# The up projection of an MLP by seven block products instead of eight

## The chip, the cores and the metric

The kernel runs on one core of one Trainium2 chip. The metric is device time in microseconds (us) of one execution, lower is better. Engines are named as in the profile: PE is TensorE's matmul, PEld its weight load, DVE is VectorE, ACT is ScalarE, POOL is GpSimd, SP issues DMAs.

## The reference, cut to what matters

One encoder block on 16 learned tokens and 512 real ones, width 2048, all in float32:

```python
h = rms_norm(h_res, norm1_g[l])
proj = h @ w_in[l]                       # 2048 x 6144
# ... short convolution on one half, neighbourhood attention on the other: mix
h_res = h_res + mix @ w_out[l]           # 2048 x 2048
h = rms_norm(h_res, norm2_g[l])
h_res = h_res + jnp.square(jax.nn.relu(h @ w_up[l])) @ w_down[l]   # 2048 x 8192, 8192 x 2048
out = rms_norm(h_res, final_norm_g)      # the 512 real tokens are returned
```

The change touches the line with `w_up` and `w_down`.

## The kernel before, in words

Every large matmul works on float32 values that are split in two: a rounded part (`hi`, written by ACT) and the remainder (`lo`, subtracted by DVE). A product is then three matmuls: hi by hi, hi by lo, lo by hi (`mm3`, lines 599 to 602, and lines 670 to 672 for the up projection). Weights arrive in slabs of 128 x 1024 values (512 KB) through `load` (SP's queue, tile `raw`), and `split` (lines 175 and 176) makes `whi` and `wlo` of them. Rings of buffers let a few slabs be loaded and split ahead of PE.

The stages stand one behind the other: projections with attention, projections with the convolution (tiles `mm_u`, `mm_c`, `mm_b`), the output projection (tiles `o_a`, `o_c`, lines 626 to 643), then the MLP. While the output projection runs, the residual stream `acc` is transposed 128 columns at a time (`transpose_h2`, tile `p2t`) and kept as `h2_hi` and `h2_lo`: 16 blocks of 128 model columns by 512 tokens.

The MLP goes in 8 chunks of 1024 hidden columns (`ch`). A chunk first makes its hidden columns: for each pair of 128-column blocks, 16 steps over the model width, each with two weight blocks and three matmuls of 128 x 512 (lines 670 to 672: 3072 matmuls in all). ACT takes relu out of PSUM, DVE squares, both split the result into `a_hi` and `a_lo`, which stay in SBUF. Then the chunk's share of the down projection follows, in four parts of 512 columns, 96 matmuls of 128 x 512 each (lines 600 to 602), and DVE adds the four banks into `acc` (line 706). PSUM has two groups of four banks (`mm`, `aux`) that take turns. The last part of the last chunk (`dl`) ends with the final norm and the stores.

The order of instructions on each engine is set by a scheduler that simulates the program; engines then run their own queues strictly in that order and wait for each other by semaphores.

Of the kernel before, what the change touches and what calls it, by code (L numbers as in the profile page):

```python
# [8 lines left out]
F32 = mybir.dt.float32  # L9
# [86 lines left out]
def hybrid_block_kernel(  # L96
# [23 lines left out]
    wp = ctx.enter_context(tc.tile_pool(name="wp", bufs=1, side="left"))  # L120
    psum = ctx.enter_context(tc.tile_pool(name="psum", bufs=4, space=bass.MemoryType.PSUM))
# [30 lines left out]
    def load(src, name):  # L152
        pool, bufs = wring["raw"].next()
        raw = pool.tile([P, SLAB], F32, tag="raw", name=f"raw_{name}", bufs=bufs)
        nc.sync.dma_start(raw, src)
        return raw

    def part_tiles(name):
        pool, bufs = wring["split"].next()
        return [pool.tile([P, SLAB], F32R, tag=t, name=f"{t}_{name}", bufs=bufs) for t in ("whi", "wlo")]  # L160
# [61 lines left out]
    with tc.tile_pool(name="p0", bufs=1, side="left") as p0:  # L222
        wring["raw"] = Ring((wp, 3, 3))
        wring["split"] = Ring((wp, 3, 2), (p0, 2, 2))
# [73 lines left out]
        wring["split"] = Ring((wp, 3, 3))  # L298
# [36 lines left out]
        wring["raw"] = Ring((wp, 3, 3))  # L335
# [242 lines left out]

    accp = ctx.enter_context(tc.tile_pool(name="accp", bufs=1, side="right"))
    acc = [accp.tile([P, D], F32, name=f"acc{t}") for t in range(NT)]  # L580
    for t in range(NT):
        nc.sync.dma_start(acc[t], x_v[t])
    h2p = tc.alloc_tile_pool(name="h2p", bufs=1, side="right")
    h2_hi = h2p.tile([P, KT, SEQ], F32R, name="h2_hi")
    h2_lo = h2p.tile([P, KT, SEQ], F32R, name="h2_lo")
    sq2 = h2p.tile([P, NT, 4], F32, name="sq2")
    rs2 = accp.tile([P, NT], F32, name="rs2")
# [19 lines left out]
    tags = ["mm", "aux"]  # L607
    turn = 0

    def transpose_h2(g):  # L610

        for t in range(NT):

            junk = h2p.tile([P, 960], mybir.dt.bfloat16, tag="junk", name=f"junk{g}_{t}")[:, :512]
            nc.scalar.activation(
                junk, acc[t][:, g * 512 : (g + 1) * 512], AF.Square, accum_out=sq2[:, t, g : g + 1]
            )
        for kt in range(4 * g, 4 * g + 4):
            pt = bank("aux", f"p2t{kt}")
            for t in range(NT):  # L620
                nc.tensor.transpose(
                    pt[:, t * P : (t + 1) * P], in_=acc[t][:, kt * P : (kt + 1) * P], identity=ident
                )
            split(h2_hi[:, kt, :], h2_lo[:, kt, :], pt, scale=g2T[:, kt : kt + 1])

    for g in range(4):
        c0 = g * 512
        for nm, xs, row, rs in halves:
            bs = [bank("mm" if nm == "a" else "aux", f"o_{nm}{c0}_{t}") for t in range(NT)]
            for s0 in range(0, 8, 2):  # L630
                wh, wl = slab(w_out[g, (row // P + s0) // 2], 512, f"o{nm}{c0}_{s0}")
                for k in range(2):
                    kt = s0 + k
                    for t in range(NT):
                        ts = slice(t * P, (t + 1) * P)
                        mm3(bs[t], xs[kt][0][:, ts], xs[kt][1][:, ts], wh[:, k, :], wl[:, k, :], kt == 0, kt == 7)
            for t in range(NT):
                a = acc[t][:, c0 : c0 + 512]
                nc.vector.scalar_tensor_tensor(a, bs[t], rs[:, t : t + 1], a, op0=ALU.mult, op1=ALU.add)

            if nm == "a" and g > 0:
                with tc.high_priority():
# [12 lines left out]
    wring["split"] = Ring((wp, 3, 3), (wp2, 3, 3))
    mp = ctx.enter_context(tc.tile_pool(name="mp", bufs=1, side="left"))
    tags = ["mm", "aux"]
    turn = 0
    for ch in range(NCHUNK):
        a_hi, a_lo = [], []  # L660
        for f in range(0, FCH, 2):
            bs = [bank(tags[turn], f"u{ch}_{f}_{i}") for i in range(2)]
            for s0 in range(0, KT, 4):
                wh, wl = slab(w_up[(ch * FCH + f) // 2, s0 // 4], 256, f"up{ch}_{f}_{s0}")
                for k in range(4):
                    kt = s0 + k
                    xh, xl = h2_hi[:, kt, :], h2_lo[:, kt, :]
                    for i in range(2):
                        h, l = wh[:, k, i * P : (i + 1) * P], wl[:, k, i * P : (i + 1) * P]
                        nc.tensor.matmul(bs[i], lhsT=h, rhs=xh, start=kt == 0, stop=False)  # L670
                        nc.tensor.matmul(bs[i], lhsT=h, rhs=xl, start=False, stop=False)  # L671
                        nc.tensor.matmul(bs[i], lhsT=l, rhs=xh, start=False, stop=kt == KT - 1)  # L672
            for i in range(2):
                r = mp.tile([P, SEQ], F32, tag="r", name=f"r{ch}_{f}_{i}", bufs=2)
# [135 lines left out]
```

## Time and profile before

| | |
|---|---|
| median of 3 runs | 2207.97 us (2207.5 to 2208.98) |
| the profiled execution | 2208.89 us, its span 2207.1 us |
| PE busy | 2192.9 us, 99% |
| DVE busy | 934.1 us, 42% |
| ACT busy | 652.2 us, 30% |
| granted TensorE clock | 0.998 of full speed |

The span runs from the first instruction to the last, and 1.8 us of the profiled execution lie outside it. Busy time says how long an engine had at least one instruction under way; on PE several matmuls are under way at once, so the duration of one and the distance from one start to the next are two different numbers.

### The profile page before, as it was taken

What the parts mean: (1) busy time and instruction counts of PE and PEld (TensorE: products, weight loads), DVE (VectorE), ACT (ScalarE), POOL (GpSimd) and SP (SyncE); (2) the same over time, 40 slices, a digit from 0 to 9 for tenths busy, and PEclk for the clock granted to TensorE, in tenths of its full rate; (3) what the DMA queues carried; (4) which work ended last, traced back from release to release, by engine and by line L of the source; (5) the groups of instructions that cost most, each with busy time, mean ns of one, the idle gap of its engine ahead of it and who ended that gap; (6) DMA issues with size and microseconds to landing.
All of it is one profiled execution on the core that took longest, in us unless ns stands there. A gap on an engine that the chain in (4) does not pass through costs nothing.

```text
span 2207.1 us, 27384 instructions
## 1 busy us (share of the span) xinstructions
PE 2192.9 (99%) x11348; PEld 1885.8 (85%) x11348; DVE 934.1 (42%) x1354; ACT 652.2 (30%) x984; POOL 143.3 (6%) x250
## 2 busy tenths in 40 slices
PE   9999999999999999999999999999999999999998
PEld 8999999999988888888888888888888888888887
DVE  6777666344334443333333333333333333333334
ACT  6455444222213333213212212212312212221323
POOL 0432221111100000000000000000000000000001
PEclk9999999999999999999999999999999999999999
DMA  5332222332363243333333333333333333333332
GB/s 196 81 91 77 82 82 77 96 95 89 95 172 91 91 143 96 96 96 98 99 100 96 96 95 96 97 100 100 96 96 96 96 97 100 99 96 96 96 105 77
DMA packets 77873, 219.00 MB, mean 99 GB/s; under 512 B 24292, under 2 KB 24372, under 8 KB 77108
## 3 DMA queue, kind: packets, MB, share of 16 engines
q1 hardware_dynamic: 77748, 217.24, 32.8%
q8 instruction: 89, 1.46, 0.3%
q14 instruction: 36, 0.29, 0.0%
HBM read 213.02 MB, written 4.19 MB: 98 GB/s over the span
## 4 chain that ended last, share of the span: by engine, by line
PE 99%; DMA 0%; ACT 0%; DVE 0%; SPq 0%; issue 0%; ACTq 0%; POOLq 0%; POOL 0%; DVEq 0%
PE u L670 11%; PE u L672 11%; PE u L671 11%; PE d L602 10%; PE d L601 10%; PE d L600 10%; PE mm_k L201 1%; PE mm_v L201 1%; PE mm_k L202 1%; PE mm_v L202 1%; PE mm_k L204 1%; PE mm_c L204 1%; PE mm_v L204 1%; PE mm_u L204 1%; PE mm_q L204 1%; PE mm_u L201 1%
## 5 line engine op out<-in xcount | busy, mean ns | idle before, releaser
L671 PE MATMUL u<-h_lo,whi_up 128*128 128x512 f32 x1024 | 398.4, 389 | 0.0
L672 PE MATMUL u<-h_hi,wlo_up 128*128 128x512 f32 x1024 | 398.4, 389 | 0.0
L670 PE MATMUL u<-h_hi,whi_up 128*128 128x512 f32 x1024 | 398.4, 389 | 0.0
L600 PE MATMUL d<-whi_dn,ah 128*128 128x512 f32 x992 | 385.9, 389 | 0.0
L601 PE MATMUL d<-wlo_dn,ah 128*128 128x512 f32 x992 | 385.9, 389 | 0.0
L602 PE MATMUL d<-whi_dn,al 128*128 128x512 f32 x992 | 385.9, 389 | 0.0
L176 DVE TENSOR_TENSOR wlo_up<-raw_up,whi_up 128x1024 fp32r<-128x1024 f32 x128 | 156.7, 1225 | 370.0 <-ACT whi_up L175 369.9
L176 DVE TENSOR_TENSOR wlo_dn<-raw_dn,whi_dn 128x1024 fp32r<-128x1024 f32 x124 | 151.9, 1225 | 369.3 <-ACT whi_dn L175 369.3
L175 ACT CAST whi_up<-raw_up 128x1024 fp32r<-128x1024 f32 x128 | 134.7, 1053 | 430.1 <-PE u L671 234.3
L175 ACT CAST whi_dn<-raw_dn 128x1024 fp32r<-128x1024 f32 x124 | 130.5, 1053 | 429.8 <-PE d L602 309.1
L672 PEld LDWEIGHTS u<-h_hi,wlo_up 128*128 128x128 f32 x1024 | 192.2, 188 | 40.0
L671 PEld LDWEIGHTS u<-h_lo,whi_up 128*128 128x128 f32 x1024 | 192.2, 188 | 39.9
L670 PEld LDWEIGHTS u<-h_hi,whi_up 128*128 128x128 f32 x1024 | 192.2, 188 | 39.8
L601 PEld LDWEIGHTS d<-wlo_dn,ah 128*128 128x128 f32 x992 | 186.2, 188 | 38.7
L600 PEld LDWEIGHTS d<-whi_dn,ah 128*128 128x128 f32 x992 | 186.2, 188 | 38.7
L602 PEld LDWEIGHTS d<-whi_dn,al 128*128 128x128 f32 x992 | 186.2, 188 | 38.6
L706 DVE SCALAR_TENSOR_TENSOR acc<-d,rs,acc 128x512 f32<-128x512 f32 x124 | 86.7, 750 | 38.9 <-PE d L602 38.9
L719 POOL TENSOR_TENSOR e<-sq 128x1 f32<-128x1 f32 x4 | 2.5, 632 | 1522.3 <-ACT junk L710 1522.3
L678 DVE TENSOR_TENSOR r<-r 128x512 f32<-128x512 f32 x64 | 44.1, 689 | 104.7 <-ACT r L677 104.7
L677 ACT ACTIVATE r<-u 128x512 f32<-128x512 f32 x64 | 38.3, 598 | 124.8 <-PE u L672 124.8
L201 PE MATMUL mm_k<-h_hi,whi_k 128*128 128x272 f32 (+1 forms) x256 | 70.0, 288 | 1.2 <-ACT whi_k L175 1.2
L201 PE MATMUL mm_v<-h_hi,whi_v 128*128 128x272 f32 (+1 forms) x256 | 69.1, 285 | 0.4 <-ACT whi_v L175 0.4
(222 smaller groups left out, 3383.1 us busy)
## 6 DMA issues: line engine op xcount, KB each, us to landing
raw_up<-in_w_up_dram SPq DMA_DIRECT2D x128, 512.0 KB
raw_dn<-in_w_down_dram SPq DMA_DIRECT2D x124, 512.0 KB
raw_q<-in_w_in_dram SPq DMA_DIRECT2D x16, 512.0 KB
raw_u<-in_w_in_dram SPq DMA_DIRECT2D x16, 512.0 KB
raw_c<-in_w_in_dram SPq DMA_DIRECT2D x16, 512.0 KB
raw_b<-in_w_in_dram SPq DMA_DIRECT2D x16, 512.0 KB
raw_oa<-in_w_out_dram SPq DMA_DIRECT2D x16, 512.0 KB
raw_oc<-in_w_out_dram SPq DMA_DIRECT2D x16, 512.0 KB
```

The source lines that it names most:

```text
L175: nc.scalar.copy(hi, src)
L176: nc.vector.tensor_tensor(lo, src, hi.bitcast(F32), op=ALU.subtract)
L201: nc.tensor.matmul(b, lhsT=wh, rhs=cols(h_hi, kt), start=kt == 0, stop=False)
L202: nc.tensor.matmul(b, lhsT=wh, rhs=cols(h_lo, kt), start=False, stop=False)
L204: last = nc.tensor.matmul(b, lhsT=wl, rhs=cols(h_hi, kt), start=False, stop=kt == KT - 1)
L600: nc.tensor.matmul(o, lhsT=ah, rhs=wh, start=start, stop=False)
L601: nc.tensor.matmul(o, lhsT=ah, rhs=wl, start=False, stop=False)
L602: nc.tensor.matmul(o, lhsT=al, rhs=wh, start=False, stop=stop)
L670: nc.tensor.matmul(bs[i], lhsT=h, rhs=xh, start=kt == 0, stop=False)
L671: nc.tensor.matmul(bs[i], lhsT=h, rhs=xl, start=False, stop=False)
L672: nc.tensor.matmul(bs[i], lhsT=l, rhs=xh, start=False, stop=kt == KT - 1)
L706: nc.vector.scalar_tensor_tensor(a, bs[t][:, :n], rs2[:, t : t + 1], a, op0=ALU.mult, op1=ALU.add)
```

## The change

The up projection is cut into 2 x 2 blocks three ways: the model width into pairs of 128 columns (8 pairs `m`), the hidden width into pairs of 128 columns (32 groups `n` of 256), the tokens into two halves of 256. Strassen's scheme (in Winograd's form) makes the four output blocks of a group from seven block products per pair instead of eight. Each product is one weight block of 128 x 128 times one operand of 128 x 256, again as three matmuls (lines 760 to 762 of the kernel after): 32 groups x 8 pairs x 7 products x 3 = 5376 matmuls of 128 x 256.

The sums that the scheme needs are made outside PE. `combine_h2` takes the place of `transpose_h2`: it scales the transposed blocks, makes four sums of them and splits all seven operands, for the 8 pairs. They lie in `sobuf` and in the tiles `xa` and `xc`, which the output projection has finished with by then. `up_slab` does the same for weights: per slab (two pairs) three sums on DVE into `tsum`, and splits of the plain blocks (`q`) and of the sums (`wsp`, 1024 columns). `up_out` combines the banks of a group by DVE, ACT applies relu and square, and the group's 512 KB go to DRAM (`a_d`). `acc` goes to DRAM too (POOL's queue), and its SBUF holds `tsum` and `q` meanwhile. The tokens are scaled before the sums (`token_scale`).

The down projection is now a phase of its own: `acc` and the groups come back from DRAM, each group is split, and the same 3072 matmuls of 128 x 512 follow.

```diff
-    def transpose_h2(g):
...
+    def combine_h2(g, tag):
+        for m in (2 * g, 2 * g + 1):
+            for e in range(2):
+                pt = bank(tag, f"p2t{2 * m + e}")
...
+                nc.vector.scalar_tensor_tensor(
+                    dst, two(pt), g2T[:, 2 * m + e : 2 * m + e + 1], two(s_bc), op0=ALU.mult, op1=ALU.mult
                 )
+            for o, a, b, op in ((4, 7, 3, ALU.subtract), (6, 0, 7, ALU.subtract), (5, 4, 0, ALU.subtract), (2, 1, 5, ALU.add)):
+                nc.vector.tensor_tensor(xq[:, o, :], xq[:, a, :], xq[:, b, :], op=op)
+            for i, j, v in places[m]:
+                split(v[:, :, 0, :], v[:, :, 1, :], xq[:, i:j, :])
+        nc.gpsimd.dma_start(acc_d[g], accs[g])
...
+    def up_slab(n, s):
+        raw = load(w_up[n, s], f"up{n}_{s}")
+        w, t = by4(raw), by4(TS.next())
+        q_hi, q_lo = (by4(v, 3) for v in Q3.next())
+        split(q_hi, q_lo, w[:, :, 1:4, :])
+        b12 = free_ap(raw[:, 0:1], [[512, 2], [0, 2], [1, P]])
+        nc.vector.tensor_tensor(t[:, :, 0:2, :], b12, w[:, :, 1:3, :], op=ALU.add)
+        nc.vector.tensor_tensor(t[:, :, 2, :], t[:, :, 0, :], w[:, :, 2, :], op=ALU.add)
+        nc.vector.tensor_tensor(t[:, :, 3, :], t[:, :, 2, :], w[:, :, 3, :], op=ALU.add)
+        t_hi, t_lo = (by4(v) for v in part_tiles(f"up{n}_{s}"))
+        split(t_hi, t_lo, t)
+        return (q_hi, q_lo), (t_hi, t_lo)
+
+    def up_step(bs, n, s):
+        both = up_slab(n, s)
+        for k in range(2):
+            m = 2 * s + k
+            for q, (sm, w, x, b, c) in PROD.items():
+                o = bs[b][:, c * HT : (c + 1) * HT]
+                h, l = (v[:, k, w, :] for v in both[sm])
+                xh, xl = (operand[m][x][:, i, :] for i in range(2))
...
+                nc.tensor.matmul(o, lhsT=h, rhs=xh, start=first, stop=False, skip_group_check=True)
+                nc.tensor.matmul(o, lhsT=h, rhs=xl, start=False, stop=False, skip_group_check=True)
+                nc.tensor.matmul(o, lhsT=l, rhs=xh, start=False, stop=m == NPR - 1, skip_group_check=True)
+
+    def up_out(bs, n):
+        e, u = E.next()
...
+        nc.scalar.copy(u[:, 0, :], bs[2][:, :HT])
+        nc.vector.tensor_tensor(u[:, 1, :], bs[0][:, :HT], u[:, 0, :], op=ALU.add)
+        nc.vector.tensor_tensor(e[:, 0, :], bs[2][:, HT:], u[:, 1, :], op=ALU.add)
+        nc.vector.tensor_tensor(e[:, 1, :], bs[3][:, :HT], u[:, 1, :], op=ALU.subtract)
+        nc.vector.tensor_tensor(e[:, 2, :], bs[3][:, :HT], e[:, 0, :], op=ALU.subtract)
+        nc.vector.tensor_tensor(e[:, 3, :], bs[0][:, HT:], u[:, 0, :], op=ALU.add)
+        nc.vector.tensor_tensor(e[:, 0:2, :], two(bs[1]), e[:, 0:2, :], op=ALU.add)
+        nc.scalar.activation(e, e, AF.Relu)
+        nc.scalar.activation(e, e, AF.Square)
+        nc.scalar.dma_start(a_d[n], e.rearrange("p s c -> p (s c)"))
...
+    accs = acc_tiles()
+    for g in range(4):
+        nc.gpsimd.dma_start(accs[g], acc_d[g])
...
+        for n in range(4 * ch, 4 * ch + 4):
+            r = AR.next()
+            nc.sync.dma_start(r, a_d[n])
+            both = A.next()
+            split(both[:, 0:1024], both[:, 1024:2048], r)
```

The first place is PE in the up projection. Before, one weight block of a slab meets `h2_hi`, `h2_lo` and again `h2_hi`, 512 tokens wide:

```order
L670 MATMUL u_2_0_8033<-h_hi,whi_up_2_12_8127 128x512
L671 MATMUL u_2_0_8033<-h_lo,whi_up_2_12_8127 128x512
L672 MATMUL u_2_0_8033<-h_hi,wlo_up_2_12_8128 128x512
L670 MATMUL u_2_1_8034<-h_hi,whi_up_2_12_8127 128x512
L671 MATMUL u_2_1_8034<-h_lo,whi_up_2_12_8127 128x512
L672 MATMUL u_2_1_8034<-h_hi,wlo_up_2_12_8128 128x512
```

After, the first group's first products on PE; `q_1` holds plain weight blocks, `sobuf` the operands, and `u_2`, `u_0`, `u_1` are banks of the group, of which each product writes one half:

```order
L760 MATMUL u_2_7889<-sobuf,q_1_7851 128x256
L761 MATMUL u_2_7889<-sobuf,q_1_7851 128x256
L762 MATMUL u_2_7889<-sobuf,q_1_7851 128x256
L760 MATMUL u_0_7887<-sobuf,q_1_7851 128x256
L761 MATMUL u_0_7887<-sobuf,q_1_7851 128x256
L762 MATMUL u_0_7887<-sobuf,q_1_7851 128x256
L760 MATMUL u_1_7888<-sobuf,q_1_7851 128x256
```

Three matmuls in a row still go to one address, now half as wide, and the weight block changes with the third and with the next product as before.

The second place is ACT where an up projection ends and a down projection begins. Before, at the last chunk (`r` is the relu out of PSUM, `ah` the rounded part of its square, `whi_dn` a slab of down weights):

```order
L677 ACTIVATE r_6_0_15819<-u_6_0_15697 128x512 [waits DVE_49,PE_49]
L175 CAST whi_dn_512_2_16014<-raw_dn_512_2_16012 128x1024 [waits DMAHW4_49,PE_49]
L677 ACTIVATE r_6_1_15826<-u_6_1_15698 128x512 [waits DVE_49,PE_49]
L175 CAST ah_6_0_15820<-r_6_0_15819 128x512 [waits DVE_49]
L175 CAST ah_6_1_15827<-r_6_1_15826 128x512 [waits DVE_49]
```

After, on ACT, the end of the last group (`u_2` is its bank; the CASTs `sobuf<-xq` split groups that have come back from DRAM, the first of them the chunk's first group):

```order
L182 CAST sobuf<-xq 128x1024 [waits DMAHW5_49]
L770 COPY ctmp<-u_2_14771 128x256 [waits PE_49]
L182 CAST wsp_dn_0_4_15088<-raw_dn_0_4_15086 128x1024 [waits DMAHW3_49,DVE_49]
L182 CAST wsp_dn_0_6_15117<-raw_dn_0_6_15115 128x1024 [waits DMAHW7_49]
L777 ACTIVATE xq<-xq 128x1024 [waits DVE_49]
L182 CAST wsp_dn_1_0_15154<-raw_dn_1_0_15152 128x1024 [waits DMAHW0_49]
L182 CAST wsp_dn_1_2_15183<-raw_dn_1_2_15181 128x1024 [waits DMAHW6_49]
L778 ACTIVATE xq<-xq 128x1024 [waits Activation_49]
L182 CAST wsp_dn_1_4_15212<-raw_dn_1_4_15210 128x1024 [waits DMAHW1_49,PE_49]
L779 DMA a_d_7886<-xq 128x1024 [waits Activation_49]
```

The relu, the square and the store of the last group now stand between casts of down weights on ACT; before, relu and cast of the last blocks had only one slab between them and nothing went to DRAM.

The third place is SP at the same point. After, the loads `xq<-a_d` bring groups back (`a_d_7857` is the chunk's third group, `a_d_7859` the next chunk's first, `a_d_7856` this chunk's second):

```order
L819 DMA xq<-a_d_7857 128x1024 [waits DMAHW5_49,DVE_49]
L159 DMA raw_dn_1_6_15239<-in_w_down_dram 128x1024 [waits DMAHW3_49,DVE_49]
L828 DMA gF<-in_final_norm_g_dram 128x2048 [waits DVE_49,PE_49]
L159 DMA raw_dn_2_0_15276<-in_w_down_dram 128x1024 [waits DMAHW7_49,DVE_49]
L159 DMA raw_dn_2_2_15305<-in_w_down_dram 128x1024 [waits DMAHW6_49,DMAHW0_49,DVE_49]
L159 DMA raw_dn_2_4_15334<-in_w_down_dram 128x1024 [waits DVE_49]
L159 DMA raw_dn_2_6_15363<-in_w_down_dram 128x1024 [waits DMAHW1_49,DVE_49]
L819 DMA xq<-a_d_7859 128x1024 [waits DMAHW2_49,DVE_49]
L819 DMA xq<-a_d_7856 128x1024 [waits DMAHW7_49,DMAHW3_49]
```

Before, SP had nothing but weight slabs (and once `gF`) there:

```order
L155 DMA raw_dn_512_0_15982<-in_w_down_dram 128x1024 [waits DMAHW6_49,DVE_49]
L155 DMA raw_dn_512_2_16012<-in_w_down_dram 128x1024 [waits DMAHW7_49,DVE_49]
L155 DMA raw_dn_512_4_16042<-in_w_down_dram 128x1024 [waits DMAHW0_49,DVE_49]
L155 DMA raw_dn_512_6_16072<-in_w_down_dram 128x1024 [waits DMAHW1_49,DVE_49]
L155 DMA raw_dn_1024_0_16118<-in_w_down_dram 128x1024 [waits DMAHW2_49,DVE_49]
```

The second group's load stands last of these, behind the slabs and behind the buffer `xq`'s half that the last up group's result leaves by DMA.

## Rows read from the trace of the kernel before

**Rows 1.** The page, parts 1 and 4: busy time and the chain.
```profile
PE 2192.9 (99%) x11348; PEld 1885.8 (85%) x11348; DVE 934.1 (42%) x1354; ACT 652.2 (30%) x984; POOL 143.3 (6%) x250
...
PE 99%; DMA 0%; ACT 0%; DVE 0%; SPq 0%; issue 0%; ACTq 0%; POOLq 0%; POOL 0%; DVEq 0%
```

**Rows 2.** Groups by line and shape on PE: busy us, mean ns of one.
```profile
L670 PE MATMUL u<-h_hi,whi_up 128*128 128x512 f32 x1024 | 398.4, 389 | 0.0
...
L204 PE MATMUL mm_u<-h_hi,wlo_u 128*128 128x256 f32 x128 | 36.1, 282 | 0.0
```

**Rows 3.** Busy us by stretch: PE, PEld, DVE, ACT, POOL, clock, DMA share, GB/s.
```profile
1200.00:1600.00 400.00, 400.00 (x1767) 331.20 (x1766) 138.58 (x147) 98.91 (x115) 0.00 (x0) 1.00 0.33 98
```

**Rows 4.** Timeline of PE, the last 48 matmuls: start us, us.
```profile
2192.23 0.28 PE L600 MATMUL dl<-whi_dlast,ah 128*128 128x256 f32 x1
2192.34 0.28 PE L601 MATMUL dl<-wlo_dlast,ah 128*128 128x256 f32 x1
...
2197.86 0.28 PE L602 MATMUL dl<-whi_dlast,al 128*128 128x256 f32 x1
```

**Rows 5.** Timeline of PE in the convolution stage, two rounds of six apart.
```profile
519.77 0.28 PE L201 MATMUL mm_u<-h_hi,whi_u 128*128 128x258 f32 x1
...
521.20 0.28 PE L201 MATMUL mm_u<-h_hi,whi_u 128*128 128x258 f32 x1
```

**Rows 6.** Groups by line and shape on DVE: busy us, mean ns of one.
```profile
L176 DVE TENSOR_TENSOR wlo_up<-raw_up,whi_up 128x1024 fp32r<-128x1024 f32 x128 | 156.7, 1225 | 370.0 <-ACT whi_up L175 369.9
...
L176 DVE TENSOR_TENSOR al<-r,ah 128x512 fp32r<-128x512 f32 x64 | 44.1, 689 | 2.8
...
L639 DVE SCALAR_TENSOR_TENSOR acc<-o_a,rs_a,acc 128x512 f32<-128x512 f32 x16 | 11.1, 749 | 3.3 <-PE o_a L602 3.3
...
L546 DVE TENSOR_TENSOR vb<-mm_c,ub 128x256 f32<-128x256 f32 x16 | 8.7, 624 | 0.0
...
L176 DVE TENSOR_TENSOR v<-pv,v 128x256 fp32r<-128x256 f32 x16 | 6.7, 418 | 6.1 <-ACT v L175 6.0
```

**Rows 7.** Groups by line and shape on ACT.
```profile
L175 ACT CAST whi_up<-raw_up 128x1024 fp32r<-128x1024 f32 x128 | 134.7, 1053 | 430.1 <-PE u L671 234.3 <-PE d L602 184.2 <-DMA raw_up<-in_w_up_dram 7.4
...
L175 ACT CAST v<-pv 128x256 fp32r<-128x256 f32 x16 | 5.9, 371 | 14.4 <-PE pv L479 13.7 <-DVE v L176 0.5
```

**Rows 8.** Timeline, 0 to 7 us: a DMA of 544 KB, its issue and its reader.
```profile
1.17 0.41 SPq L248 DMA_DIRECT2D xT<-in_xT_dram  x1
...
5.02 1.76 ACT L178 ACTIVATE h_hi<-xT,g1T 128x272 fp32r<-128x272 f32 x4 [2.81 <-DMA xT<-in_xT_dram]
```

**Rows 9.** Busy us by stretch, as rows 3: the stretch with most DMA traffic.
```profile
10.00:20.00 10.00, 9.74 (x76) 9.31 (x75) 10.00 (x22) 10.00 (x24) 0.00 (x0) 1.00 1.03 406
```

**Rows 10.** Timeline of PE around its longest wait.
```profile
32.94 0.40 PE L202 MATMUL mm_q<-h_lo,whi_q 128*128 128x512 f32 x1
35.25 0.50 PE L204 MATMUL mm_q<-h_hi,wlo_q 128*128 128x512 f32 x1 [1.92 <-DVE wlo_q L176]
...
36.80 0.63 PE L202 MATMUL mm_q<-h_lo,whi_q 128*128 128x512 f32 x1
37.22 0.63 PE L204 MATMUL mm_q<-h_hi,wlo_q 128*128 128x512 f32 x1
...
39.36 0.50 PE L202 MATMUL mm_q<-h_lo,whi_q 128*128 128x512 f32 x1
39.70 0.39 PE L204 MATMUL mm_q<-h_hi,wlo_q 128*128 128x512 f32 x1
```

**Rows 11.** Busy us by stretch, as rows 3: behind that wait.
```profile
36.00:38.00 2.00, 2.00 (x6) 1.57 (x6) 2.00 (x3) 0.00 (x0) 0.00 (x0) 0.54 0.82 236
```

**Rows 12.** Timeline of PE: transposes between matmuls of the output projection.
```profile
761.66 1.80 PE L621 MATMUL p2t<-ident,acc 128*128 128x128 f32 x15
```

More of the change, by code (lines that the diff above doesn't have):

```diff
@@ L158, in part_tiles @@
     def part_tiles(name):
-        pool, bufs = wring["split"].next()
-        return [pool.tile([P, SLAB], F32R, tag=t, name=f"{t}_{name}", bufs=bufs) for t in ("whi", "wlo")]
+        both = wring["split"].next(name)
+        return both[:, :SLAB], both[:, SLAB:]
+    raw_slots = lambda n, pool: pool_slots(n, pool, [P, SLAB], F32, "raw")
+    split_slots = lambda n, pool: pool_slots(n, pool, [P, 2 * SLAB], F32R, "wsp")
     def parts(raw, b, name):
@@ new lines, in token_scale @@
+    def token_scale():
+        nc.vector.tensor_scalar(ms0, sq2[:, :, 0], 1.0 / 512, EPS, op0=ALU.mult, op1=ALU.add)
+        nc.gpsimd.tensor_tensor(s0, ms0, mhalf[:, :NT], op=ALU.pow)
+        ps = bank("aux", "ps")
+        for t in range(NT):
+            diag = h2p.tile([P, P], F32, tag="diag", name=f"diag2{t}", bufs=2)
+            nc.vector.tensor_scalar_mul(diag, ident, s0[:, t : t + 1])
+            nc.tensor.matmul(ps[:, t * P : (t + 1) * P], lhsT=ones2, rhs=diag, start=True, stop=True)
+        nc.vector.tensor_copy(s_bc, ps)
@@ new lines, in hybrid_block_kernel @@
+    banks = lambda n: [bank(("mm", "aux")[n % 2], f"u{n}_{i}") for i in range(4)]
+    first = [banks(n) for n in range(2)]
+    for n in range(2):
+        for s_ in range(3):
+            up_step(first[n], n, s_)
+    for n in range(2):
+        up_step(first[n], n, 3)
+        up_out(first[n], n)
+    for n in range(2, NG):
+        bs = banks(n)
+        for s_ in range(4):
+            up_step(bs, n, s_)
+        up_out(bs, n)
+    accs = acc_tiles()
+    for g in range(4):
+        nc.gpsimd.dma_start(accs[g], acc_d[g])
@@ L660, in hybrid_block_kernel @@
         a_hi, a_lo = [], []
[L661 to L674, printed above, removed]
-                ah = mp.tile([P, SEQ], F32R, tag="a_hi", name=f"ah{ch}_{f}_{i}", bufs=FCH)
-                al = mp.tile([P, SEQ], F32R, tag="a_lo", name=f"al{ch}_{f}_{i}", bufs=FCH)
-                nc.scalar.activation(r, bs[i], AF.Relu)
-                nc.vector.tensor_tensor(r, r, r, op=ALU.mult)
-                split(ah, al, r)
-                a_hi.append(ah)
-                a_lo.append(al)
@@ L701, in hybrid_block_kernel @@
+        if last:
+            nc.sync.dma_start(gF, final_g.partition_broadcast(P))
+        for i in range(3 if last else 4):
+            bs = [bank(tags[turn], f"d{ch}_{i}_{t}") for t in range(NT)]
+            turn ^= 1
+            for s_ in range(0, FCH, 2):
+                wh, wl = slab(w_down[i, (k0 + s_) // 2], 512, f"dn{ch}_{i}_{s_}")
+                for k in range(2):
+                    kt = s_ + k
                     for t in range(NT):
-                        ts = slice(t * P, (t + 1) * P)
@@ L743, in hybrid_block_kernel @@
         for i in range(4):
[L744 to L745 removed]
+            o = acc(i, t)
             if i % 2:
```

175 lines of the change are left out of this document (104 added, 71 removed).

## The prediction, made before the changed kernel was run

> **What bounds the kernel now.** I read the busy times and the chain of waits first [rows 1]. PE is busy 99% of the span and the chain is PE from end to end, so anything that PE does less of comes straight off the time, and whatever another engine does counts only where it makes PE wait. The next thing is what one matmul costs. The groups by line give 389 ns for a 128x512 matmul and 282 ns for a 128x256 one [rows 2], and it is tempting to multiply counts by these. That would be wrong: 1024 matmuls of 389 ns in each of three lines make 1195 us for the up projection alone, and the same again for the down projection, more than the span holds. A duration runs from a matmul's start to its result; several are under way at once. What fills the time is the distance from start to start. In a stretch that holds only 128x512 matmuls of the MLP, 1767 of them start in 400 us [rows 3]: 0.2264 us each. For 128x256 the nearest rows are the last 48 matmuls, which also go three in a row to one address as in the changed kernel: 5.63 us from the first start to the 48th [rows 4], so 0.1198 us each. In the convolution stage, with widths of 258 and 256 and two addresses that alternate, twelve starts take 1.43 us [rows 5], 0.1192 us each. I take 0.1198.
>
> From these two points, a matmul costs 0.416 ns for each column and 13.2 ns besides (226.4 less 119.8 is 106.6 ns for 256 columns).
>
> **The up projection on PE.** Removed are 3072 matmuls of 128x512: 3072 x 0.2264 = 695.5 us. Added are 5376 of 128x256: 5376 x 0.1198 = 644.0 us (640.8 by rows 5). An eighth of the columns is saved, 81.9 us, and 2304 more matmuls cost 30.4 us of fixed share. Net: 51.5 us less. The scheme pays as long as the fixed share is under 81.9 / 2304 = 35.5 ns.
>
> The Trainium skill ("TensorE: Matmul & The Clock Gate", section "Back-to-back issue gap") speaks against such a change: it gives about 81 ns for each matmul of 128 columns and 131 ns for one of 512 in a stream with weight loads, so time hardly falls with the width. By an estimate from these figures (98 ns at 256) the up projection would cost 124 us more than by the same page's 131 ns. The trace does not agree with it: 226.4 ns and 119.8 ns.
>
> **Whether the other engines keep up.** A group of the up projection has 168 matmuls, 20.1 us of PE, where a group's worth took 21.7 us before. DVE is given much more work. Per slab: the remainder of 768 columns, which I put between 689 ns at 512 and 1225 ns at 1024, 0.96 us; sums of 512, 256 and 256 columns, 0.69 + 2 x 0.42 us; the remainder of 1024, 1.23 us [rows 6]. That is 3.7 us, four times 14.9. At the end of a group five combinations of 256 and one of 512 out of PSUM add 2.8 us. DVE needs 17.7 us of PE's 20.1, where it was busy 35% of the time before [rows 3]. ACT has 4 x (0.83 + 1.05) for casts (768 columns between the rows for 256 and 1024), 0.4 for the copy, 2.1 for relu and square at the price of a cast of 1024 [rows 7]: 10.0 us. DMA moves 2.6 MB per group, 130 GB/s, where 98 were moved before [rows 3] and 406 have been seen [rows 9]. Rings of three slabs let splits run two slabs, 10 us, ahead of PE, and a group's banks need not be free until the group after next. So I cost DVE, ACT and DMA in the steady state at nothing; the cover is thin on DVE only, 2.4 us of each group. If the sums, whose operands are strided, cost what the strided addition of 256 columns does (624 ns instead of 418 [rows 6]), each slab takes 0.75 us more, DVE 20.7 us, and 32 groups lose 0.6 us each: 19 us.
>
> **The output projection.** The scaled sums of `combine_h2` cost DVE per pair two reads of PSUM at 0.75, four sums at 0.42 and a remainder of 1792 columns at about 2 us [rows 6]: 5.2 us, 10.4 per 512 columns, in a stretch where PE spends 2 x 21.7 us and DVE has had half its time free. They lie beside the matmuls. `token_scale` adds four small matmuls at 0.12 us [rows 12] to PE: 0.4 us. The 16 transposes of the last quarter stay on PE, after the start of the up projection now instead of before it.
>
> **The start of the up projection.** PE has the operands of six of eight pairs by then. The third slab's plain blocks go where `acc`'s last megabyte lay, which leaves by a DMA of POOL's queue, a kind with no row here. PE wants that slab after two slabs and 16 transposes, 10.1 + 1.9 us; cast and remainder take 1.8 and the last addition into `acc` 0.75. The write may last 9.4 us without loss. It takes 2.6 us at the highest rate seen and 10.7 at the mean rate [rows 3, 9], and what POOL's queue adds is unknown; behind the waiting cast on ACT stand those of the next slabs and of the last two pairs' operands. Between 0 and 8 us lost; I take 2, near the middle of the two rates.
>
> **The seam between up and down.** Before, the down projection began with hidden columns split long ago, and PE never stopped there. Now the first chunk's second group needs the half of `xq` out of which the last group's result is stored. Count from PE's last up matmul. ACT copies (0.4 us), DVE makes its combinations with one remainder of weights among them (2.8 + 1.2), so relu starts at 4.4. On ACT's queue relu (1.05), two casts of weights, square, another cast and then the store follow: the store is issued at about 9.7 us. A DMA of 544 KB took 3.9 us from issue to its reader [rows 8]; 512 KB out and back therefore end at 17.4, the cast at 18.5. PE meanwhile has the first group's matmuls for two parts, 48 x 0.2264 = 10.9 us, and between them waits 1.1 us for the cast of the second part's weights, the one behind the relu. It then idles until 18.5: 6.5 us. Such a wait costs something afterwards: before PE's longest wait of 1.92 us matmuls ran at full clock, and some 1 us after it eight came 0.43 us apart [rows 10], with a granted clock of 0.54 [rows 11], so at the 1.2 GHz level of the two. Eight times 0.2 is 1.6 us. Together 9.2; `acc` comes back by four megabytes of DMA at the same time, so I take 10. Bounds: 4, if both transfers run at 406 GB/s (1.3 us each); 20, if they queue behind the 4 MB (10 us at that rate).
>
> The down projection itself keeps its 3072 matmuls of 128x512 and the tail behind it.
>
> **The sum**, against the profiled execution: 2207.1 - 695.5 + 644.0 + 0.4 + 2 + 10 = 2168.0 us of span, and 1.8 us outside it: 2169.8. That execution is 0.9 us above the median of the runs, so the forecast for the median is **2169 us**, 1.8% faster.
>
> **Rivals.**
> 1. *DVE and ACT take turns and set the pace.* A slab's remainder of sums needs ACT's cast, and that needs DVE's sums. If DVE stands still during each such cast, a slab takes 3.7 + 1.05 us and a group 4 x 4.77 + 2.8 + 0.4 = 22.3 us instead of 20.1. Times 32, 70 us more: 2239, slower than before. It decides from 21.3 us a group on ((695.5 - 12.4) / 32). For it: DVE's load doubles, and it was idle before nearly every remainder until ACT's cast came [rows 6]. Against it: that idling was spare time of an engine with nothing else to do, the sums of the next slab need no cast and can fill it, and in the stretch with most work DVE was busy 10.0 us of 10 [rows 9].
> 2. *The fixed share of a matmul counts in full*, that is, durations and not starts: 5376 x 0.282 - 3072 x 0.389 = 321 us more, 2530. Against it stand rows 3 to 5: starts lie closer than durations. The page named above would put its time on this side too.
> 3. *The seams are dear.* With 20 us at the seam and 8 at the start instead of 12: 2185, still faster. For it: two DMA round trips on the path whose issue stands at the end of full queues; against it, DMA is two thirds idle in the MLP [rows 3].
>
> **How the numbers follow.** My forecast has 0.74, its own range 2155 to 2180: at the low end 640.8 for the matmuls, no loss at the start and 4 at the seam (2158, and a few us for what the scheduler moves elsewhere). Rival 3 has 0.12 (2180 to 2198), the strided sums or a little of rival 1 on top of it 0.04 (about 2198 to 2212), rival 1 has 0.08, rival 2 has 0.02. The range that should hold 8 times in 10 is 2154 to 2198: its top is the forecast with the 19 us of strided sums and 10 more at the seam. What a measurement here can tell from no change is 0.2%, 4.4 us. Faster by more than that: the forecast, rival 3 and a little of the case between, 0.87. Within it: 0.03. Slower: rivals 1 and 2, 0.10.
>
> **What the changed profile would show.** In the middle of the up projection 168 matmuls in 20.1 us, 0.1198 us apart, PE without idle time, DVE busy 85 to 90%. If PE idles there on a `wsp` or `q` of DVE, rival 1 is at work; the stretch per group then reads over 20.1 us. At the seam PE should idle about 6 us on a cast of ACT with a DMA behind it, and the clock should read about half for some 3 us after it; at the start of the up projection a wait on the third slab's `q` should be 0 to 8 us. The rest of the span should be as before within 1 or 2 us. I am wrong if matmuls of 256 columns come at another distance in the new setting, where operands lie in other tiles and each product writes half a bank, or if PE's waits in the up projection add up to more than 30 us.

## The result, and the profile after

The changed kernel takes 2173.63 us (median of 4 runs, 2171.55 to 2175.9); the kernel before took 2208.46 beside it. The ratio is 0.9843, 95% interval 0.9826 to 0.986: 1.6% faster. A second set of runs gave 2174.46 and a ratio of 0.9845 (0.9831 to 0.9858). The forecast was 2169, its range 2154 to 2198. The profiled execution took 2175.9, with a span of 2174.1 where 2168.0 was worked out.

The page of the changed kernel, parts 1 and 4, answers to [rows 1]:

```profile
PE 2148.8 (99%) x13660; PEld 1959.9 (90%) x13660; DVE 1292.1 (59%) x2015; ACT 798.1 (37%) x1110; POOL 142.1 (7%) x260
...
PE 98%; DMA 1%; ACT 0%; DVE 0%; SPq 0%; issue 0%; ACTq 0%; POOLq 0%; POOL 0%; DVEq 0%
```

PE still fills the span, with 2312 more matmul records and 44 us less time. DVE has 358 us more and still isn't on the chain. The middle of the up projection by stretch answers to [rows 3], columns as there:

```profile
1000.00:1200.00 200.00, 200.00 (x1669) 200.00 (x1669) 167.06 (x259) 97.37 (x110) 0.00 (x0) 1.00 0.38 130
```

200 us by 1669 is 0.1198 us a matmul, as taken from [rows 4], at full clock, without an idle moment. (The count takes in two matmuls that had started before the window; by the 1667 starts in it, the distance is 0.1200.) DVE is busy 84%, DMA moves 130 GB/s. The additions and remainders of a weight slab, on DVE by line and shape, answer to [rows 6]:

```profile
L183 DVE TENSOR_TENSOR wsp_up<-tsum,wsp_up 128x1024 fp32r<-128x1024 f32 x128 | 156.4, 1222 | 49.7 <-ACT wsp_up L182 45.7
...
L183 DVE TENSOR_TENSOR q<-raw_up,q 128x768 fp32r<-128x768 f32 x128 | 122.4, 956 | 34.7 <-ACT q L182 34.6
L744 DVE TENSOR_TENSOR tsum<-raw_up 128x512 f32<-128x512 f32 x128 | 88.0, 689 | 4.0 <-DMA raw_up<-in_w_up_dram 1.2
...
L746 DVE TENSOR_TENSOR tsum<-tsum,raw_up 128x256 f32<-128x256 f32 x128 | 54.0, 422 | 2.9
```

No strided sum costs more than a plain one: 689 and 422 ns. The wait for ACT's cast that stood before nearly every remainder is there in part (45.7 and 34.6 us), in time that DVE has to spare.

What is lost is lost at the seam. PE, last up matmul, the two waits, and the matmuls behind them:

```profile
1452.59 0.28 PE L762 MATMUL u<-xc_hi,wsp_up 128*128 128x256 f32 x1
1452.71 0.40 PE L630 MATMUL d<-wsp_dn,sobuf 128*128 128x512 f32 x1
...
1460.62 1.81 PE L630 MATMUL d<-wsp_dn,sobuf 128*128 128x512 f32 x4 [2.28 <-ACT wsp_dn L182]
...
1476.40 0.79 PE L630 MATMUL d<-wsp_dn,sobuf 128*128 128x512 f32 x1 [8.45 <-ACT sobuf L182]
1476.99 0.63 PE L631 MATMUL d<-wsp_dn,sobuf 128*128 128x512 f32 x1
1477.42 0.63 PE L630 MATMUL d<-wsp_dn,sobuf 128*128 128x512 f32 x1
...
1481.57 0.40 PE L630 MATMUL d<-wsp_dn,sobuf 128*128 128x512 f32 x1
```

And the same stretch by windows, columns as [rows 3]:

```profile
1456.00:1460.00 4.00, 2.34 (x11) 1.61 (x9) 2.41 (x4) 2.48 (x3) 0.00 (x0) 1.00 1.00 416
1460.00:1464.00 4.00, 3.38 (x9) 2.62 (x10) 2.92 (x3) 4.00 (x5) 0.00 (x0) 0.62 1.04 432
...
1468.00:1472.00 4.00, 0.00 (x0) 0.00 (x0) 0.53 (x1) 1.04 (x1) 0.00 (x0) 0.90 1.04 423
1472.00:1476.00 4.00, 0.00 (x0) 0.00 (x0) 1.56 (x2) 1.74 (x2) 0.00 (x0) 0.50 0.87 334
```

PE idles twice, 2.28 and 8.45 us, and after each wait matmuls start 0.43 us apart for most of some 4 to 5 us, at a clock of 0.5 to 0.62, the 1.2 GHz level for all or part of it. Until the second wait ends, DMA has a share of 0.87 to 1.04. I measure the seam's loss, here and below, as the time from the first down matmul to one some 40 to 50 us later, less 0.2264 us for each matmul between: 15.35 us, of which 10.7 are the two waits and 4.6 the lower clock and small change.

What DMA moves there, by queue (packets, MB, share of the 16 engines; q0 is POOL's queue, q1 SP's, q10 ACT's), from 1456 to 1460 us:

```profile
q0 software_dynamic: 125, 0.90, 53.3%
q1 hardware_dynamic: 215, 0.76, 46.6%
```

and from 1462.5 to 1470, while the last group's store (q10) is under way:

```profile
q1 hardware_dynamic: 527, 2.37, 83.6%
q10 hardware_dynamic: 144, 0.52, 17.1%
```

The last megabyte of `acc` was asked for at 1451.73 and had landed at 1460.4, 2 us before the store was issued at 1462.51. So the store did not run beside `acc`, but beside what SP asked for around that time: the final gains (1 MB, at 1456.23), four weight slabs (1458.81 to 1464.70) and another hidden group (1465.83).

### The profile page after: what moved, and what is told of

It reads as the page before. It is cut to its first block, busy times and chain, and to the rows that moved or that the text cites. A ratio compares the mean times of both kernels' runs of the same rounds, so it can differ in the third digit from the quotient of the medians.

```text
span 2174.1 us, 33195 instructions
## 1 busy us (share of the span) xinstructions
PE 2148.8 (99%) x13660; PEld 1959.9 (90%) x13660; DVE 1292.1 (59%) x2015; ACT 798.1 (37%) x1110; POOL 142.1 (7%) x260
## 4 chain that ended last, share of the span: by engine, by line
PE 98%; DMA 1%; ACT 0%; DVE 0%; SPq 0%; issue 0%; ACTq 0%; POOLq 0%; POOL 0%; DVEq 0%
PE d L630 10%; PE d L631 10%; PE d L632 10%; PE u L762 10%; PE u L761 10%; PE u L760 10%; PE mm_v L208 1%; PE mm_v L211 1%; PE mm_v L209 1%; PE mm_k L211 1%; PE mm_k L209 1%; PE mm_k L208 1%; PE mm_u L211 1%; PE mm_c L211 1%; PE mm_q L211 1%; PE mm_u L208 1%
## 5 line engine op out<-in xcount | busy, mean ns | idle before, releaser
L630 PE MATMUL d<-wsp_dn,sobuf 128*128 128x512 f32 x992 | 387.8, 392 | 10.7 <-ACT sobuf L182 8.5
L631 PE MATMUL d<-wsp_dn,sobuf 128*128 128x512 f32 x992 | 387.9, 391 | 0.0
L632 PE MATMUL d<-wsp_dn,sobuf 128*128 128x512 f32 x992 | 384.8, 390 | 0.0
L183 DVE TENSOR_TENSOR wsp_dn<-raw_dn,wsp_dn 128x1024 fp32r<-128x1024 f32 x124 | 151.7, 1224 | 293.0 <-ACT wsp_dn L182 293.0
L182 ACT CAST wsp_dn<-raw_dn 128x1024 fp32r<-128x1024 f32 x124 | 130.5, 1053 | 395.9 <-PE d L632 379.7
L630 PEld LDWEIGHTS d<-wsp_dn,sobuf 128*128 128x128 f32 x992 | 187.3, 189 | 50.5 <-ACT sobuf L182 8.9
L631 PEld LDWEIGHTS d<-wsp_dn,sobuf 128*128 128x128 f32 x992 | 187.4, 189 | 39.2 <-DVE wsp_dn L183 0.2
L632 PEld LDWEIGHTS d<-wsp_dn,sobuf 128*128 128x128 f32 x992 | 186.6, 188 | 38.9
L183 DVE TENSOR_TENSOR wsp_up<-tsum,wsp_up 128x1024 fp32r<-128x1024 f32 x128 | 156.4, 1222 | 49.7 <-ACT wsp_up L182 45.7
L182 ACT CAST wsp_up<-tsum 128x1024 fp32r<-128x1024 f32 x128 | 134.2, 1049 | 69.5 <-PE u L762 64.7
L760 PE MATMUL u<-sobuf,wsp_up 128*128 128x256 f32 x512 | 145.0, 283 | 0.0
L761 PE MATMUL u<-sobuf,wsp_up 128*128 128x256 f32 x512 | 145.0, 283 | 0.0
L762 PE MATMUL u<-sobuf,wsp_up 128*128 128x256 f32 x512 | 144.6, 283 | 0.0
L183 DVE TENSOR_TENSOR q<-raw_up,q 128x768 fp32r<-128x768 f32 x128 | 122.4, 956 | 34.7 <-ACT q L182 34.6
L761 PE MATMUL u<-sobuf,q 128*128 128x256 f32 x384 | 108.7, 283 | 0.0
L760 PE MATMUL u<-sobuf,q 128*128 128x256 f32 x384 | 108.5, 283 | 0.0
L762 PE MATMUL u<-sobuf,q 128*128 128x256 f32 x384 | 108.5, 283 | 0.0
L760 PEld LDWEIGHTS u<-sobuf,wsp_up 128*128 128x128 f32 x512 | 98.3, 192 | 0.0
L761 PEld LDWEIGHTS u<-sobuf,wsp_up 128*128 128x128 f32 x512 | 98.3, 192 | 0.0
L762 PEld LDWEIGHTS u<-sobuf,wsp_up 128*128 128x128 f32 x512 | 98.2, 192 | 0.0
```

Of the source, the lines that this page charges most:

```text
L182: nc.scalar.copy(hi, src)
L183: nc.vector.tensor_tensor(lo, src, hi.bitcast(F32), op=ALU.subtract)
L630: nc.tensor.matmul(o, lhsT=ah, rhs=wh, start=start, stop=False)
L631: nc.tensor.matmul(o, lhsT=ah, rhs=wl, start=False, stop=False)
L632: nc.tensor.matmul(o, lhsT=al, rhs=wh, start=False, stop=stop)
L760: nc.tensor.matmul(o, lhsT=h, rhs=xh, start=first, stop=False, skip_group_check=True)
```

## The experiments

**The changed kernel again** (no edit).

> The changed kernel once more, as it is, beside the three kernels that follow. Its second trace tells which of its losses come back: the seam between up and down (about 15 us in the first trace: idle 2.3 and 8.5 us and some 4 us of matmuls at the lower clock), and the 1.7 us by which it was already late after the first 35 us. If the seam's size is set by transfers that queue behind the 4 MB of acc, it should vary by a few us between executions, 12 to 17; if it is a fixed chain of instructions, it should be the same within 1 us. The 1.7 us at the beginning should be gone or different if they are a matter of the execution, and the same if the changed kernel's first stage is built differently. Time: 2172 to 2175.

Measured: 2174.46 us; seam 15.7 us, waits of 2.3 and 8.2. So the seam is no accident of one execution: it varied by 0.4 us, not by a few. By the yardstick of the expectation that spoke for a fixed chain of instructions; the runs below show that the traffic has a part as well, so the yardstick was too coarse. The beginning is another matter. Busy us from 0 to 20 us, first trace:

```profile
0.00:20.00 20.00, 16.67 (x98) 15.68 (x99) 13.10 (x30) 14.51 (x32) 0.80 (x9) 0.91 0.89 329
```

and second:

```profile
0.00:20.00 20.00, 17.18 (x114) 15.85 (x115) 13.87 (x32) 15.28 (x34) 0.80 (x9) 1.00 0.89 331
```

In the first the clock fell early, in the second not, and the q projection began at 32.4 us instead of 34.3 (32.6 before). Over all fourteen traces of this study, the kernel before among them, the up projection starts between 801.7 and 805.9 us. Those 1.7 us (805.9 against 804.2 in the second trace) belong to the execution.

**acc read back late.** The four loads go from before the seam to behind the second group's cast, by a dependency on it.

```
-    for g in range(4):
-        nc.gpsimd.dma_start(accs[g], acc_d[g])
...
             split(both[:, 0:1024], both[:, 1024:2048], r)
+            if n == 1:
+                for g in range(4):
+                    nc.gpsimd.tensor_copy(accs[g][:, 0:1], both[:, 0:1].bitcast(F32))
+                    nc.gpsimd.dma_start(accs[g], acc_d[g])
```

> The 4 MB of acc are read back only once the second hidden group of the first chunk has been cast, and so not during the seam. Theory (the seam cost more than the forecast because DMA was full: the last group's store and its load took 7.3 and 5.4 us instead of 3.9 each): both go back to about 4 us, PE's longest wait falls from 8.5 to 3 to 4 us, the first wait (2.3 us, for weights whose DMA was late) goes as well, and the time falls by 5 to 7 us to about 2167. Rival (the order of ACT's and SP's queues sets the chain, whatever DMA does): wait and time stay within 1.5 us of the changed kernel. What could spoil it: acc's first megabyte is wanted about 35 us after the seam's start and is asked for some 20 us after it.

Measured: 2172.5 us, 1 to 2 less; seam 14.35. A miss: the first wait went, but the other grew to 11.5 us. DVE in that stretch shows one reason (from the last group's first combination to its last, L771 to L776):

```profile
1453.86 0.42 DVE L771 TENSOR_TENSOR ctmp<-u,ctmp 128x256 f32<-128x256 f32 x1
1454.19 0.42 DVE L775 TENSOR_TENSOR xq<-u,ctmp 128x256 f32<-128x256 f32 x1
1454.53 1.22 DVE L183 TENSOR_TENSOR wsp_dn<-raw_dn,wsp_dn 128x1024 fp32r<-128x1024 f32 x1
...
1456.32 1.22 DVE L183 TENSOR_TENSOR sobuf<-xq,sobuf 128x1024 fp32r<-128x1024 f32 x1
1457.45 0.42 DVE L774 TENSOR_TENSOR xq<-u,xq 128x256 f32<-128x256 f32 x1
1457.79 1.22 DVE L183 TENSOR_TENSOR wsp_dn<-raw_dn,wsp_dn 128x1024 fp32r<-128x1024 f32 x1
1458.92 0.69 DVE L776 TENSOR_TENSOR xq<-u,xq 128x512 f32<-128x512 f32 x1
```

Weights that arrive earlier are also split earlier, and three remainders (two of weights, one of a hidden group) now stand between the combinations, with two more ahead of them. The store is issued 11.3 us after the first down matmul (9.8 in the changed kernel). The store took 5.3 us instead of 7.4, and its load 4.5 to 4.9 instead of 5.4: shorter, though `acc` had landed before the store in the changed kernel too, and still longer than 3.9, for DMA stays full without it (408 GB/s from 1460 to 1464 us). With `acc` ahead of them the next five weight slabs were asked for between 2.8 and 12 us after the first down matmul, without it between 1 and 8.5; so `acc` lengthened the store, as I read it, by pushing weights into its time. About 3 us gained, 1.5 lost by the later issue: the rest is what the seam shows. Both readings hold a part; the rival had named the queues of ACT and SP, and it was DVE's as well.

**The same, in order.** The later weights' casts are also kept behind the last group's store (`stored`).

```
...
-                wh, wl = slab(w_down[i, (k0 + s_) // 2], 512, f"dn{ch}_{i}_{s_}")
+                raw = load(w_down[i, (k0 + s_) // 2], f"dn{ch}_{i}_{s_}")
+                late = ch == 0 and (i > 1 or s_ > 0)
+                with tc.issue_after(stored.ins) if late else nullcontext():
+                    wh, wl = parts(raw, 512, f"dn{ch}_{i}_{s_}")
```

> As the run with acc read back late, and the casts and remainders of the first chunk's weights (all but the first slabs) also kept behind the store of the last group's result. In that run DVE did five remainders between the combinations, the result's relu began 9.1 us after the last up matmul instead of 4.4, and the store was issued at 11.3. Theory (two things make the seam: the length of the two transfers, and what stands ahead of the store in the queues of DVE and ACT): the store is now issued at about 6.5 us, lands 5 us later, the load takes 4 more and cast 1, so the second group is there at about 17 us; the first 48 matmuls take 10.9, the lower clock 1.6 to 2.5; lost at the seam 7 to 9 us instead of 14.4, and 2165 to 2168. Price: the second part's weights are cast later, so the wait is split in two. Rival (order matters little, the transfers alone set the end): lost 12 us or more, 2170 or over.

Measured: 2164.64 us (2164.6 to 2166.11), seam 7.6. ACT (relu, store, cast of the second group) and, last, SP's issue of that group's load:

```profile
1453.36 1.06 ACT L777 ACTIVATE xq<-xq 128x1024 f32<-128x1024 f32 x1 [1.90 <-DVE xq L776]
...
1455.54 0.33 ACTq L779 DMA_DIRECT2D a_d<-xq  x1
...
1462.19 1.05 ACT L182 CAST sobuf<-xq 128x1024 fp32r<-128x1024 f32 x1 [0.51 <-DMA xq<-a_d]
```

```profile
1458.65 0.33 SPq L817 DMA_DIRECT2D xq<-a_d  x1
```

With the first down matmul at 1449.09, relu begins at 4.3 us and the store is issued at 6.5. The store takes 3.1 us, the load 3.5, a little under the 3.9 of [rows 8]: with the casts held back no ring buffer comes free, and SP asks for no weight slab between 1444.62 and 1459.07. It is the weights, then, that slowed the store and the load in the changed kernel, perhaps with the gains, which are asked for 5 us earlier here (1451.18). The second group is there at 14 us; what PE waits for now, 5.1 us, is the second part's weights, cast behind three others. So the second group's way is the length of two transfers plus what stands ahead of the store, and both terms can be moved.

**The other half.** The first chunk's four groups come back through the half of `xq` that the last group doesn't use.

```
-    AR = Ring(*[lambda name, i=i: part(flat(xq), 1024, i) for i in range(2)])
+    AR = Ring(*[lambda name, i=i: part(flat(xq), 1024, i) for i in [0, 0, 0, 0] + [1, 0] * 14])
```

> The first chunk's four hidden groups all come back through that half of xq which the last group but one has left, so the second group no longer waits until the last group's result is stored. acc is still read back in the seam. Theory (the wait on the store of the last group is the seam's largest term): PE's wait of 8.5 us and the lower clock behind it go, some 9 to 11 us, and 2164 is left; the first wait of 2.3 us, for weights, stays. Rival (with DMA full the third group, which now goes through the same half after the second, is as late as the second was): a wait of 4 to 8 us turns up a few matmuls later and the time falls by less than 5 us.

> The first chunk through the other half, alone, once more, beside the run above. Time 2159 to 2163, seam 4.3 us; its first trace was at the MLP 2.5 us earlier than most others, because the lower clock behind PE's first long wait did not come, and this should vary from execution to execution.

Measured: 2160.93 us (2159.22 to 2161.15), ratio 0.9782 (0.9769 to 0.9796); again 2161.88, ratio 0.9789 (0.9775 to 0.9802). The seam is 4.3 and 4.0 us. PE's two longest waits of the first of these traces, us in total, times, longest:

```profile
PE d L630 <- ACT wsp_dn L182: 2.3, 1, 2.3
PE mm_q L211 <- DVE wsp_q L183: 1.9, 1, 1.9
```

The 8.45 us are gone with the lower clock behind them, 11 us of seam for a change of buffer numbers. Of the 12.7 us of time, the first trace's early start (2.5 us) is a part; it did not come again in the second.

**Both edits**, and both with the fourth group, or the other half alone with the fourth group, through the last group's half (`[0, 0, 0, 1] + [0, 1] * 14`).

> Both edits: the first chunk through the other half of xq, and acc read back only after the second group's cast. If the two losses are what the theory says, PE waits less than 1.5 us in all at the seam, and the time is 2173.6 less about 14, 2158 to 2161: matmuls alone, with the loss of the beginning. If something else ends the wait (weights behind a full ring, ACT's order), 3 us or more of the seam stay, 2163 or over.

> As the run with both edits, but the first chunk's fourth hidden group comes back through the half that the last group of the up projection leaves, so that it need not wait until the third has been cast. In that run PE still waited 2.1 us, behind 144 matmuls of the down projection, for a cast of a hidden group. Theory: that wait goes, and the seam costs under 1 us: 2160 to 2162. Rival: the wait is the third group's, which still goes through the same half, and stays: no change. Beside it: all runs so far reach the first matmul of the MLP between 801.7 and 805.9 us, whatever is changed behind it; this range of 4 us is the execution's own and limits what can be told apart here.

> As the run in which the first chunk comes back through the other half (acc read back in the seam), but with the fourth group through the half of the last one. Seam there: 4.3 us, of which 2.4 a wait for weights whose transfer was late and 1.6 the lower clock behind it. Theory (that wait is DMA traffic, not the hidden groups): seam and time as there, 4 to 5 us and 2159 to 2163. Rival: fewer transfers in a row through one half start the weights earlier, and the seam is under 2 us.

Measured: 2162.63 us with a seam of 2.9; 2163.27 (2162.84 to 2169.54) with 10.8 in its trace, which is of the longest execution; 2161.28 with 4.7, as expected. No gain over the other half alone, in time, and the first two missed their forecasts (2158 to 2161, and 2160 to 2162). In the first of the three the third group's load (SP) and its cast (ACT) show what acc does at its new place:

```profile
1458.15 0.33 SPq L817 DMA_DIRECT2D xq<-a_d  x1
```

```profile
1472.10 1.05 ACT L182 CAST sobuf<-xq 128x1024 fp32r<-128x1024 f32 x1 [2.53 <-DMA xq<-a_d]
```

Fourteen us for 512 KB, among 4 MB of acc that POOL asked for from 1456.67 on and 1 MB of gains from 1457.06. In the second it is 16.4 us, and PE waits 2.7 us for the third group and 3.0 for the fourth. Moved in one piece, the burst had only changed its victim. The expectation for the second (that the wait for the fourth group goes) is refuted, and the third comes late besides; this trace alone shows it, and in the other executions, some 6 us shorter, the waits may be smaller.

**The burst spread.** The other half, acc asked for in three portions, the gains in the last chunk.

```
+            for g in {1: (0,), 2: (1,), 3: (2, 3)}.get(n, ()):
+                nc.gpsimd.tensor_copy(accs[g][:, 0:1], both[:, 0:1].bitcast(F32))
+                nc.gpsimd.dma_start(accs[g], acc_d[g])
...
+            nc.gpsimd.tensor_copy(gF[:, 0:1], both[:, 0:1].bitcast(F32))
             nc.sync.dma_start(gF, final_g.partition_broadcast(P))
```

> The first chunk through the other half, and the 4 MB of acc not in one piece but a megabyte behind the second group's cast, one behind the third's and two behind the fourth's; the final gains (1 MB) are loaded in the last chunk instead of in the seam. In the runs with all of acc behind the second group's cast, the third group's load stood among 5 MB of other transfers and took 14 to 16 us, and PE waited for it and for the fourth. Theory (the seam is set by the burst, wherever it is put): the loads of the third and fourth group take 3 to 6 us, no wait of PE in the seam is over 1 us, the seam costs under 1.5 us, and the time is 2158 to 2161, at or below the best so far. Rival (the waits come from the order of SP's queue or from taking turns in one half of xq): a wait of 2 us or more remains, 2161 to 2164.

Measured: 2158.22 us (2157.13 to 2158.96), ratio 0.9772 (0.9759 to 0.9786), seam 0.1 us. All that PE waits for in the whole program:

```profile
PE mm_q L211 <- DVE wsp_q L183: 1.9, 1, 1.9
PE pg L239 <- POOL ident masks.py:199: 1.4, 1, 1.4
PE mm_k L208 <- ACT wsp_k L182: 0.6, 1, 0.6
PE pg L273 <- DVE g1T L271: 0.3, 1, 0.3
```

No wait of the MLP is left. The third group's load took 7.0 us (1 more than expected), the fourth's 3. This version is faster than both kernels. That `acc` and the gains were moved together leaves open which of the two counts for how much.

**Half-width matmuls without the scheme.** The kernel before, its up projection's matmuls each in two halves.

```
+                        for v in range(2):
+                            cs = slice(v * 256, v * 256 + 256)
+                            o, yh, yl = bs[i][:, cs], xh[:, cs], xl[:, cs]
...
```

> The kernel before, with each 128x512 matmul of the up projection issued as two of 128x256, nothing else changed: the eight block products without the scheme, so that only the fixed share of a matmul is added. By the two distances, 6144 x 0.1198 less 3072 x 0.2264 is 40.6 us more: 2249. Rival (durations or a fixed gap count: 282 against 389 ns): 6144 x 0.282 less 3072 x 0.389 is 537 us more. Third reading (the distance in the changed kernel is short only because successive products use several banks): here a bank is written three times in a row as there, so a distance over 0.125 us would have to come from elsewhere.

Measured: 2249.14 us beside 2208.88, 40.3 more (ratio 1.018, 1.0163 to 1.0197). Its duration per matmul, 283 ns, is that of [rows 2] again, and again it isn't what time follows:

```profile
L674 PE MATMUL u<-h_lo,whi_up 128*128 128x256 f32 x2048 | 579.7, 283 | 0.0
```

The fixed share, 3072 x 13.2 ns, is measured by itself. From here to the changed kernel 768 matmuls of 0.1198 us go, 92 us, and the seam takes 15 back.

**More work for DVE.** The addition of 512 columns in each slab done twice, and three times.

```
         nc.vector.tensor_tensor(t[:, :, 0:2, :], b12, w[:, :, 1:3, :], op=ALU.add)
+        nc.vector.tensor_tensor(t[:, :, 0:2, :], b12, w[:, :, 1:3, :], op=ALU.add)
```

> The changed kernel with the addition of 512 columns in each weight slab of the up projection done twice: 4 x 0.69 = 2.8 us more of DVE per group. DVE was busy 167 of 200 us, 16.8 of a group's 20.1; it goes to 19.5, 97%. Theory (DVE's work lies beside PE's as long as it is less than 20.1 us a group): no more than 5 us slower, PE without waits in the middle of the up projection. Rival (DVE and ACT take turns, so that a good part of DVE's idle time can't be used): the group grows by up to 2.8 us, 30 to 88 us slower.

> The same addition done three times: 5.5 us more of DVE per group, 22.3 us against PE's 20.1. Theory: DVE now sets the pace, 2.2 us a group, 32 times: 70 us slower than the changed kernel, about 2244, and PE waits for the remainders of the weights. If DVE and ACT also take turns, the group is longer than 22.3 us and the time over 2250; if ACT's waits leave DVE idle at all, its busy share in the middle stays under 100%.

Measured: 2176.71 us, 2 to 3 more, with 1.6 us of it in the up projection and some 1.5 at the seam, where PE now waits 14.3 us before the first down matmul; and 2241.95, some 68 more, 65 of them in the up projection. The middle of the up projection, twice:

```profile
1000.00:1200.00 200.00, 200.00 (x1669) 200.00 (x1668) 180.70 (x299) 92.81 (x109) 0.00 (x0) 1.00 0.37 130
```

and three times:

```profile
1000.00:1200.00 200.00, 191.48 (x1519) 183.96 (x1518) 185.64 (x308) 85.62 (x99) 0.00 (x0) 1.00 0.36 120
```

```profile
PE u L762 <- ACT wsp_up L182: 27.7, 60, 1.3
```

The cover was real: 18.2 us of DVE per group still hide. With the second repeat a group takes 168 / 1519 x 200 = 22.1 us, as expected, but not by the sum I made. DVE's busy time rises only to 20.5 us a group, as back-to-back instructions overlap, and the other 1.6 are waits for casts and loads: the taking of turns that rival 1 spoke of, which begins to cost somewhere between 18.2 and 20.5 us of DVE work.

## Why the prediction was right, and where it was off

- **The distance, not the duration: right.** From the first up matmul to the first down matmul it is 646.85 us, in every trace of this up projection without added work. 644.0 were worked out for its matmuls; the 16 transposes that lie in this stretch, as they did before, take 1.8 at 0.11 us each, and the last 1 us is 0.1200 us a matmul instead of 0.1198. The net of 51.5 us stood: from the first up matmul to the end of the span, with the seam's loss taken off, the changed kernel is 51.0 us shorter.
- **The cover on DVE: right**, at 16.8 us a group instead of 17.7, without the price of strided sums. Rival 1 was rightly a rival: one addition per slab was covered, two were not.
- **The output projection:** 0.9 us longer instead of 0.4. The four small matmuls of `token_scale` stand in the trace as eight, at 0.11 to 0.12 us each; they are also why there are 2312 more matmul records and not 2304. That the 16 transposes changed their side of the MLP's start was wrong; they stood behind it before as well, which cost nothing.
- **The start of the up projection: 0 instead of 2.** PE never waited. By the page acc's stores land 4.5 us after their issue in the median; 9.4 were free.
- **The seam is the step that was mis-sized: 15.4 us instead of 10.** Its mechanism came as written: relu at 4.7 us (4.4), store issued at 9.8 (9.7). Then the store took 7.4 us and the load 5.4, where I had 3.9 for each from a stretch with little else under way. The bound of 20 was for transfers that queue behind `acc`, and I took a value near that of the quiet row. What they met was not `acc`, which had landed by then, but weight slabs and gains that became possible at the same moment; the prediction has no price for these. The first wait was 2.3 us for 1.1, since the weights came late (it went when `acc` was asked for later), and two waits meant two stretches of lower clock, 4.6 us instead of 1.6. What the parts are worth, the runs show: without the wait on the last group's store 11 of the 15.4 us go (the other half), with `acc` spread and the gains moved besides the other 4; `acc` moved alone took 1.
- **The beginning:** 1.7 us of the profiled execution's 6.1 us over the worked-out span are an early fall of the clock that the second trace doesn't have. The rest is the seam's 5.4, half a us each of the output projection and of the net, less the 2 at the start.
- **Rival 3** (2185, seams of 28 us in all) lay further off than the forecast, though its argument, round trips behind full queues, was the right one for what went wrong. Rival 2 is refuted by the half-width run. The figures of the Trainium skill ("TensorE: Matmul & The Clock Gate", "Back-to-back issue gap"), by an estimate from which the narrow matmuls would have cost more than the wide ones saved, don't hold here: 226.4 ns at 512 columns, and 119.8 to 120.0 at 256 in three settings ([rows 4], the changed kernel, the half-width run).

## What to carry to other kernels

Trade matmul width against count by start-to-start distances, not by durations. Where one phase hands over to another, add up every transfer that becomes possible at that moment, and price each round trip at the traffic of that stretch; then look for a buffer that lets the first pieces go early, and spread what isn't wanted yet. Here a burst that was moved as one piece only moved the wait.

## What the runs showed of the hardware that was not expected

- DVE's instructions overlap: in the run with one addition doubled, an addition of 0.42 us started 0.33 to 0.34 us before the next. Sums of durations overstate DVE by some 5% in the changed kernel (17.6 against 16.8 us a group) and by 11% in that run (20.2 against 18.2).
- A 512 KB store or load took 3.1 to 3.5 us once acc was out of the way and the later weights held back, 4.5 to 7.4 beside weight slabs and gains, and 14 to 16 among the 5 MB of acc and gains.
- At 256 columns the weight loads fill the time as well: PEld 200.00 of 200 us in the up projection, against 331 of 400 at 512 columns [rows 3]. Whether narrower matmuls would still follow the straight line was not tried. The only full ones of 128 columns in these traces, the transposes [rows 12], start 0.11 us apart, where the line gives 0.066; they are another kind of matmul, so this is a hint and no more.
- After PE's first long wait (1.9 us at 35 us) the clock fell in eleven of the fourteen traces, mean 0.93 to 0.94 from 35 to 60 us, and in three it didn't (1.00; among the traces of the changed kernel and its variants, these start the up projection first, at 801.7 to 802.2 us). Nor did it fall behind the wait of 2.1 us in the run with both edits, at 1486 us, while it did behind one of 1.8 us in the second run of the other half. What decides it stays open.
